# Nine norm factors spread over the partitions through DRAM instead of by TensorE, in a two-layer decoder on one core

## The chip, the core and the metric

The kernel runs on one core of a Trainium2 chip. Its metric is the device time in microseconds (us) of one execution, as a median of runs; lower is better. PE is TensorE (its matmuls; PEld its weight loads), DVE is VectorE, ACT is ScalarE, POOL is GpSimd, SP is SyncE. "Stage" below is a slab of weights of at most 1024 columns that is loaded, split and multiplied as one.

## The reference

Two layers on a sequence of 256 tokens with 2048 features, all in float32. Layer 0 mixes tokens by a state-space scan (SSD), layer 1 by attention with a forget gate (FoX). Both then have a gated feed-forward part of 5632 features and a gated extra input. Every part stands between root-mean-square norms:

```python
def rmsnorm(x, w):
    y = xf * lax.rsqrt(jnp.mean(xf * xf, axis=-1, keepdims=True) + EPS)
    return y * w
...
    y = y.reshape(b, l, SSD_D_INNER) * jax.nn.silu(z)      # SSD mixer
    yg = y.reshape(b, l, g, SSD_D_INNER // g)              # 8 groups of 512
    yg = yg * lax.rsqrt(jnp.mean(yg * yg, axis=-1, keepdims=True) + EPS)
    y = yg.reshape(b, l, SSD_D_INNER) * norm_w
    return y @ w_out
```

The change concerns nine of these norms: the eight group norms in the SSD mixer (the "gate norms", one for each group of 512 features) and the norm ahead of FoX's input product. Each has one factor per token, 256 in all.

## The kernel before, in words

Activations lie transposed, features on partitions and 256 tokens along the free dimension, as tiles of 128 x 256. All products are made to float32 precision from two float32r halves: a weight tile `raw` comes by DMA on SP's queue (L194), ACT rounds it to `wh` (L208), DVE makes the rest `wl = raw - wh` (L213), and PE makes three products for each weight block of 128 x 128 (L269 to L271, or L263 to L265 where tokens are the stationary side, as for FoX's V). Six accumulators (`acc`, in PSUM) rotate, four of them to a unit of 512 output features; two more PSUM tiles (`mi`) serve the small products.

A unit runs over its stages. After each stage one task is popped from a list `bg`, so that the small work of one unit runs beside the products of the next. In the SSD layer units alternate: `xs_unit(g+1)` makes the scan's input of group g+1 (its accumulators are read by DVE at L299 as `xr<-acc`), `z_unit(g)` makes the gate of group g (`g<-acc`, L299). `core_tasks` is the scan of a group: decays `E` on ACT (L1001, L1008) and DVE (L1009), the transposed input `xd` (DVE, L986), their products on PE (L1021). `gate_tasks` is the gate norm. The program's order on each engine is made by a scheduler from the order of the code, its own timing model and the pins `issue_after`: `after(low_a[0])` puts an instruction behind the last emitted `wh` cast, `paced` puts one behind the last emitted `wl` and ahead of the next.

A norm has three steps. `rstd_small` (L349): PE sums the squares over the partitions by using the 128 x 256 tile of squares as stationary side, 128 tokens at a time, against a column of ones (L352), which leaves the factor of token 128 j + p on partition p, column j; DVE scales it (`ms`, L355), GpSimd takes it to the power -1/2 (`rs`, L358). `rstd_wide` (L361): DVE splits the two columns into `rh` and `rl` (L363, L364), PE spreads each column over all partitions by four products of 128 columns (L368), and ACT copies the result out of PSUM (L372), for the gate norms as `grw`. Then the factors are used: for a gate norm by `gn3` (L1055), four operations of DVE that scale `y` (L1058). In `gate_tasks` the steps are `gn1`, `gn2`, `gn3`, one stage after the other; for the last two groups `gn3` is pinned and comes in the output product (`last7`, L1142). For FoX's norm the steps are made by `mk_r` (L544) and run inside V's second unit; `rwide` and `rq = rwide * FOXS` (L1266) are first used when the `q` and `k` units are read out.

Of the kernel before, what the change touches and what calls it, by code (L numbers as in the profile page):

```python
# [65 lines left out]
def tile_trunk(ctx, tc, a, out):  # L66
# [4 lines left out]
    def pool(stack, name, bufs=1, **kw):  # L71
        return stack.enter_context(tc.tile_pool(name=name, bufs=bufs, **kw))
# [10 lines left out]
    gap = pool(ctx, "gap")  # L83
    psa = pool(ctx, "psa", bufs=6, space=PSUM)
    psm = pool(ctx, "psm", bufs=2, space=PSUM)

    cnt = [0]

# [203 lines left out]
    def misc():  # L292
        return psm.tile([P, 512], F32, tag="mi", name=nm("mi"))
# [52 lines left out]
        turn.append(last_v[0])  # L346
        return r

    def rstd_small(acc, n):  # L349
        ps = misc()  # L350
        for j in range(2):
            PE.matmul(ps[:, j:j + 1], lhsT=acc[:, j * P:(j + 1) * P], rhs=ones[:, :1],  # L352
                      start=True, stop=True)
        ms = tmp("ms", (P, 2))
        dmark[0] = V.tensor_scalar(out=ms, in0=ps[:, :2], scalar1=1.0 / n, scalar2=EPS,  # L355
                                   op0=mult, op1=add)
        rs = tmp("rs", (P, 2), bufs=3)
        G.tensor_tensor(out=rs, in0=ms, in1=mhalf, op=ALU.pow)  # L358
        return rs

    def rstd_wide(rs, o):  # L361
        rr = [tmp("rh", (P, 2), F32R), tmp("rl", (P, 2), F32R)]
        V.tensor_copy(out=rr[0], in_=rs)  # L363
        dmark[0] = V.tensor_tensor(out=rr[1], in0=rs, in1=rr[0].bitcast(F32), op=sub)  # L364
        ps = misc()
        for j in range(2):
            for i in range(2):
                PE.matmul(ps[:, j * P:(j + 1) * P],  # L368
                          lhsT=rr[i][:, j:j + 1].broadcast_to((P, P)), rhs=identr,
                          start=i == 0, stop=i == 1)  # L370
        if o is not None:
            mark[0] = A.copy(out=o, in_=ps[:, :T])  # L372
        return ps[:, :T]

    def log1p_exp_neg_abs(v, new):
        ab = new()
# [164 lines left out]
                emit_stage(hi, prev[0])  # L541
        return up

    def mk_r(half=True, small=None):  # L544
        r = []

        def f1():
            r.append(rstd_small(ssb, D))
            if small is not None:
                V.tensor_copy(out=small, in_=r[0])  # L550

        def f2():
            rstd_wide(r[0], rwide)
            if half:
                V.tensor_scalar(out=rwide2, in0=rwide, scalar1=0.5, scalar2=None, op0=mult)
        return f1, f2

    def mk_r_paced():
# [266 lines left out]
    with ExitStack() as ys:  # L825
        yp = pool(ys, "yp", side="right")
        y = [yp.tile([P, T], F32, name=f"y{c}") for c in range(32)]
        with ExitStack() as st:
# [136 lines left out]
            def core_tasks(g, xg):  # L965
# [26 lines left out]
                def decay(q, half):  # L992
                    h0 = 8 * g + 4 * q
                    ab = S[f"a{q}"]
                    if half == 0:
                        S[f"E{q}"] = s3[0].tile([P, 4, 384], F32, tag="E", name=nm("E"), bufs=2)
                    E = S[f"E{q}"]
                    with after(low_a[0]):
                        for i in range(2 * half, 2 * half + 2):
                            for b, lo in ((0, 0), (1, P), (2, P)):  # L1000
                                A.activation(E[:, i, b * P:(b + 1) * P], ab[:, i, lo:lo + P],  # L1001
                                             AF.Relu, scale=-1.0,
                                             bias=bias3[:, b, h0 + i:h0 + i + 1])
# [35 lines left out]
                def ymm_y():  # L1039
                    ymm()  # L1040
                    y_of(1)

                return [lambda: decay(0, 0), lambda: decay(0, 1), xpose, lambda: decay2(0),
                        lambda: decay(1, 0), lambda: decay(1, 1), lambda: decay2(1), noop, ymm_y,
                        lambda: y_of(0), noop]

            def gate_tasks(g, S):
                def gn1():
                    S["rs"] = rstd_small(S["ss"], 512)

                def gn2():
                    S["rw"] = yp.tile([P, T], F32, tag="grw", name=nm("grw"), bufs=1)
                    rstd_wide(S["rs"], S["rw"])

                def gn3():  # L1055
                    for c in range(4):
                        yc = y[4 * g + c]
                        last_v[0] = V.scalar_tensor_tensor(out=yc, in0=yc, scalar=col("ssd_norm", 4 * g + c),  # L1058
                                               in1=S["rw"], op0=mult, op1=mult)
                if g < NG - 2:  # L1060
                    return [noop, gn1, gn2, gn3]
                late.append(lambda: paced(gn3))
                return [noop, gn1, gn2] if g < NG - 1 else [gn1, noop, gn2, noop]

            xgs, late, later, last7 = {}, [], [], []
            zt = {}

            def z_a(t):
# [41 lines left out]
            def z_unit(g, pops):  # L1110
                S = {}

                def ev_z(t, acc):
                    if t == 0:
                        while len(bg) > left[0]:
                            bg.popleft()()
                    if t == 0:
                        S["ss"] = ssp
                        if g == 0:
                            gated(0, z00, z00)  # L1120
                    if g == 0:
                        t += 1
                    yc = y[4 * g + t]
                    if g == NG - 1:
                        later.append((acc, yc, S["ss"]))
                        return
                    z = tmp("g0")
                    gated(t, acc, z)

                def gated(t, src, z):  # L1130
                    yc = y[4 * g + t]
                    gather_with(src, z, rwide2)
                    th = tmp("th")
                    A.activation(th, z, AF.Tanh)
                    V.scalar_tensor_tensor(out=z, in0=th, scalar=1.0, in1=z, op0=add, op1=mult)
                    V.tensor_tensor(out=yc, in0=yc, in1=z, op=mult)
                    sumsq(S["ss"], yc, t == 0)
                unit(lambda k: xs0[k], ev_z, pops=pops)
                if g < NG - 1:
                    bg.extend(gate_tasks(g, S))  # L1140
                else:
                    last7.extend([late[0]] + gate_tasks(g, S) + [late[1]])  # L1142

            xs_unit(0)
            for g in range(NG - 1):
# [10 lines left out]
                bg.append(lambda c=c: ysplit(c))  # L1156
            left[0] = 0
            z_unit(NG - 1, 2)
        xq_s = ExitStack()
        xq = pool(xq_s, "xq", bufs=16)  # L1160
        zp = pool(xq_s, "zp")
# [4 lines left out]
            later[t] = (z, yc, ss)  # L1166
        turn.append(took[0][1])
        low[0] = took[0][1]
        bg.extend([lambda j=j: z_step(j) for j in range(6)] + last7)
        st0 = {}  # L1170

        def m0():
# [79 lines left out]
                            in1=bigm.unsqueeze(1).broadcast_to((P, 4, P)), op=add)  # L1252
        return ck

    v1, v2 = mk_r(False, rsm)

    def both(t, acc):
        if t == 0:
# [3 lines left out]
    for u in range(1, 5):  # L1262
        unit(lambda k: nxt[k], both if u == 1 else ev_v(u), tok=True,
             late=(lambda: (drain(), v1()), v2) if u == 1 else ())
        if u == 1:
            V.tensor_scalar(out=rq, in0=rwide, scalar1=float(FOXS), scalar2=None, op0=mult)  # L1266
    bg.extend((f1, noop, f2, noop, f3))
    ots = {}

# [177 lines left out]
```

## Time and profile before

| what | before |
|---|---|
| median of 3 runs | 2702.18 us (2701.43 to 2702.31) |
| the profiled execution | 2703.08 us, its span 2701.3 us |
| PE busy | 2695.0 us, 23302 matmuls |
| DVE, ACT, POOL busy | 1782.0, 1395.5, 46.7 us |
| granted TensorE clock | full (1.000) |
| DMA queues: SP's; GpSimd's; ACT's | 504.54 MB; 12.15 MB; 0.14 MB |

The span runs from the first instruction to the last; the execution has some 2 us around it. A float32 product that is not float32r (L352, L1021) leaves two records for each matmul. Matmuls overlap in the trace, so that their cost is read from start to start, and not from their durations.

### The profile page before, as it was taken

What the parts mean: (1) busy time and instruction counts of PE and PEld (TensorE: products, weight loads), DVE (VectorE), ACT (ScalarE), POOL (GpSimd) and SP (SyncE); (2) the same over time, 40 slices, a digit from 0 to 9 for tenths busy, and PEclk for the clock granted to TensorE, in tenths of its full rate; (3) what the DMA queues carried; (4) which work ended last, traced back from release to release, by engine and by line L of the source; (5) the groups of instructions that cost most, each with busy time, mean ns of one, the idle gap of its engine ahead of it and who ended that gap; (6) DMA issues with size and microseconds to landing.
All of it is one profiled execution on the core that took longest, in us unless ns stands there. A gap on an engine that the chain in (4) does not pass through costs nothing. (4 is left out here: it accounts for less than half of the span.)

```text
span 2701.3 us, 56196 instructions
## 1 busy us (share of the span) xinstructions
PE 2695.0 (100%) x23302; PEld 2679.6 (99%) x23302; DVE 1782.0 (66%) x2747; ACT 1395.5 (52%) x2156; POOL 46.7 (2%) x108
## 2 busy tenths in 40 slices
PE   9999999999999999999999999999999999999999
PEld 9999999999999999999999999999999999999999
DVE  8788888754966545666568656656865545656577
ACT  6577666554644444444446544455644444444455
POOL 0000000000000000000000000000000000000000
PEclk9999999999999999999999999999999999999999
DMA  7666666565666666666656676655766666666655
GB/s 267 188 205 200 191 195 190 161 216 172 193 205 195 193 193 193 195 178 203 200 164 209 183 224 185 179 159 173 204 203 194 195 195 193 193 179 210 195 166 171
DMA packets 262736, 520.42 MB, mean 193 GB/s; under 512 B 17440, under 2 KB 44224, under 8 KB 262480
## 3 DMA queue, kind: packets, MB, share of 16 engines
q1 hardware_dynamic: 258784, 504.54, 62.3%
q0 software_dynamic: 3552, 12.15, 1.5%
q8 instruction: 182, 2.98, 0.4%
q14 instruction: 74, 0.61, 0.1%
q10 hardware_dynamic: 144, 0.14, 0.0%
HBM read 514.58 MB, written 2.18 MB: 191 GB/s over the span
## 5 line engine op out<-in xcount | busy, mean ns | idle before, releaser
L213 DVE TENSOR_TENSOR wl<-raw,wh 128x1024 fp32r<-128x1024 f32 (+4 forms) x1020 | 1173.2, 1152 | 751.1 <-ACT wh L208 749.8
L208 ACT CAST wh<-raw 128x1024 fp32r<-128x1024 f32 (+4 forms) x1020 | 1011.3, 994 | 1116.8 <-PE acc L270 991.4
L270 PE MATMUL acc<-x,wh 128*128 128x256 f32 x5120 | 1392.0, 277 | 0.0
L271 PE MATMUL acc<-x,wl 128*128 128x256 f32 x5120 | 1365.3, 276 | 0.0
L269 PE MATMUL acc<-x,wh 128*128 128x256 f32 x5120 | 1356.9, 277 | 0.0
L270 PEld LDWEIGHTS acc<-x,wh 128*128 128x128 f32 x5120 | 960.9, 188 | 2.1 <-issue 1.9
L271 PEld LDWEIGHTS acc<-x,wl 128*128 128x128 f32 x5120 | 948.3, 188 | 0.8 <-issue 0.7
L269 PEld LDWEIGHTS acc<-x,wh 128*128 128x128 f32 x5120 | 936.7, 188 | 1.1 <-issue 0.9
L270 PE MATMUL acc<-a,wh 128*128 128x256 f32 x1408 | 388.2, 276 | 0.0
L269 PE MATMUL acc<-a,wh 128*128 128x256 f32 x1408 | 388.0, 276 | 0.0
L271 PE MATMUL acc<-a,wl 128*128 128x256 f32 x1408 | 385.4, 275 | 0.0
L270 PEld LDWEIGHTS acc<-a,wh 128*128 128x128 f32 x1408 | 264.4, 188 | 0.0
L269 PEld LDWEIGHTS acc<-a,wh 128*128 128x128 f32 x1408 | 264.2, 188 | 0.0
L271 PEld LDWEIGHTS acc<-a,wl 128*128 128x128 f32 x1408 | 263.5, 188 | 0.0
L269 PE MATMUL acc<-xb,wh 128*128 128x256 f32 x512 | 143.8, 281 | 0.5 <-DVE qk L299 0.5
L270 PE MATMUL acc<-xb,wh 128*128 128x256 f32 x512 | 141.4, 276 | 0.0
L271 PE MATMUL acc<-xb,wl 128*128 128x256 f32 x512 | 140.6, 276 | 0.0
L269 PEld LDWEIGHTS acc<-xb,wh 128*128 128x128 f32 x512 | 96.1, 188 | 1.2 <-DVE qk L299 0.9
L270 PEld LDWEIGHTS acc<-xb,wh 128*128 128x128 f32 x512 | 96.2, 188 | 0.2
L271 PEld LDWEIGHTS acc<-xb,wl 128*128 128x128 f32 x512 | 95.8, 188 | 0.2 <-issue 0.2
L917 DVE SCALAR_TENSOR_TENSOR g<-xr,vec,g 128x256 f32<-128x256 f32 x144 | 66.3, 478 | 8.5 <-ACT g L914 7.9
L269 PE MATMUL acc<-xq,wh 128*128 128x256 f32 x256 | 70.7, 276 | 0.0
(217 smaller groups left out, 1979.4 us busy)
## 6 DMA issues: line engine op xcount, KB each, us to landing
raw<-down SPq DMA_DIRECT2D x176, 512.0 KB, 3.7
raw<-ssd_in SPq DMA_DIRECT2D x144, 512.0 KB, 4.2
raw<-gate SPq DMA_DIRECT2D x128, 512.0 KB, 3.7
raw<-up SPq DMA_DIRECT2D x128, 512.0 KB, 3.7
raw<-fox_in SPq DMA_DIRECT2D x64, 512.0 KB, 4.2
raw<-gate SPq DMA_DIRECT2D x64, 384.0 KB, 3.3
raw<-up SPq DMA_DIRECT2D x64, 384.0 KB, 3.6
raw<-ssd_out SPq DMA_DIRECT2D x40, 512.0 KB, 3.7
```

The lines of the kernel that those rows point to most:

```text
L208: low_a[0] = A.copy(out=wh, in_=raw)
L213: low[0] = V.tensor_tensor(out=wl, in0=raw, in1=wh.bitcast(F32), op=sub)
L269: PE.matmul(o, lhsT=w, rhs=x[:, 0, :], start=st, stop=False)
L270: PE.matmul(o, lhsT=w, rhs=x[:, 1, :], start=False, stop=False)
L271: last = PE.matmul(o, lhsT=wl[:, c, t * P:(t + 1) * P], rhs=x[:, 0, :], start=False, stop=sp)
L917: V.scalar_tensor_tensor(out=c, in0=xr[:, k:k + T], scalar=col(f"conv_w{k}", cc), in1=c, op0=mult, op1=add)
```

## The change

The factors of the nine norms no longer go through PE, DVE's split and ACT's copy. GpSimd writes the two columns of `rs` to a scratch tile in DRAM behind the power (`sent`), and ACT's DMA queue fetches them from there to all 128 partitions (`fetched`), pinned behind a `wh` cast. The scalings `gn3` are pinned as well. `gn2` and `gn3` of a group are put on a second list `scale`, from which `core_tasks` of a later group takes one entry at its fourth and one at its eighth step.

```diff
-    def rstd_small(acc, n):
+    def rstd_small(acc, n, woven=False):
         ps = misc()
+        if woven:
+            halves_ = acc.rearrange("p (q j) -> p j q", j=2)
+        else:
+            halves_ = acc.rearrange("p (j q) -> p j q", j=2)
         for j in range(2):
-            PE.matmul(ps[:, j:j + 1], lhsT=acc[:, j * P:(j + 1) * P], rhs=ones[:, :1],
+            PE.matmul(ps[:, j:j + 1], lhsT=halves_[:, j, :], rhs=ones[:, :1],
                       start=True, stop=True)
...
+    def sent(rs, woven):
+        d = rp.tile([2 * P], F32, tag="rsd", name=nm("rsd"), bufs=2)
+        G.dma_start(out=d.rearrange("(p j) -> p j" if woven else "(j p) -> p j", j=2), in_=rs)
+        return d
+
+    def fetched(d, o):
+        with after(low_a[0]):
+            A.dma_start(out=o, in_=d.partition_broadcast(P))
...
-                return [lambda: decay(0, 0), lambda: decay(0, 1), xpose, lambda: decay2(0),
-                        lambda: decay(1, 0), lambda: decay(1, 1), lambda: decay2(1), noop, ymm_y,
+                return [lambda: decay(0, 0), lambda: decay(0, 1), xpose,
+                        lambda: (next_scale(), decay2(0)),
+                        lambda: decay(1, 0), lambda: decay(1, 1), lambda: decay2(1), next_scale, ymm_y,
                         lambda: y_of(0), noop]
...
                 def gn1():
-                    S["rs"] = rstd_small(S["ss"], 512)
+                    S["rs"] = sent(rstd_small(S["ss"], 512, True), True)
...
-                    rstd_wide(S["rs"], S["rw"])
+                    fetched(S["rs"], S["rw"])
...
                 if g < NG - 2:
-                    return [noop, gn1, gn2, gn3]
-                late.append(lambda: paced(gn3))
-                return [noop, gn1, gn2] if g < NG - 1 else [gn1, noop, gn2, noop]
+                    return [noop, gn1, lambda: scale.extend((gn2, lambda: paced(gn3))), noop]
+                late.append((gn2, lambda: paced(gn3)))
+                return [noop, gn1, noop] if g < NG - 1 else [gn1]
...
-                    last7.extend([late[0]] + gate_tasks(g, S) + [late[1]])
+                    last7.extend([late[0][1]] + gate_tasks(g, S) + [noop] * 4
+                                 + [late[1][0]] + [noop] * 3 + [late[1][1]])
...
-        bg.extend([lambda j=j: z_step(j) for j in range(6)] + last7)
+        bg.extend([lambda j=j: (z_step(j), late[0][0]() if j == 1 else None)
+                   for j in range(6)] + last7)
...
-    v1, v2 = mk_r(False, rsm)
+    def v2():
+        rs_v.append(sent(rs_v[0], False))
+
+    def scale_q():
+        last_v[0] = V.tensor_scalar(out=rq, in0=rwide, scalar1=float(FOXS), scalar2=None, op0=mult)
...
         if u == 1:
-            V.tensor_scalar(out=rq, in0=rwide, scalar1=float(FOXS), scalar2=None, op0=mult)
+            bg.extend([noop] * 5 + [lambda: fetched(rs_v[1], rwide)] + [noop] * 4
+                      + [lambda: paced(scale_q)])
```

With `woven` the stationary side of L352 takes every second token, so that the factor of token 2 p + j stands on partition p, column j, and a partition's two factors lie side by side in DRAM.

The scheduler orders the SSD layer's instructions anew. PE's queue has 36 matmuls fewer (the nine calls of L368), and its other rows keep their number. The products with `E` and `xd` of the fifth group stand behind 2921 plain products in the changed order, and behind 2911 before. Lines of the changed kernel are numbered up to 30 higher.

ACT's queue, fifth gate norm. `wh` is a stage's cast, `E` the decays, `th` and `g` belong to the convolution of the next group. Before, the copy of the factors stands among the casts:

```order
L208 CAST wh_5505<-raw_5503 128x1024
L208 CAST wh_5539<-raw_5537 128x1024
L372 COPY grw_5492<-mi_5497 128x256
L208 CAST wh_5621<-raw_5619 128x1024
L1001 ACTIVATE E_5649<-ab_5611,bias_219 128x128 x6
L914 ACTIVATE g_423_5570<-xr_5567,vec 128x256
```

In the changed order the fetch stands later in the same unit, ahead of the exponential:

```order
L209 CAST wh_5655<-raw_5653 128x1024
L931 ACTIVATE th_5536<-g_412_5531 128x256
L931 ACTIVATE th_5547<-g_415_5542 128x256
L209 CAST wh_5698<-raw_5696 128x1024
L387 DMA grw_5726<-rsd_5436 128x256
L1019 ACTIVATE E_5610<-E_5610 128x1536
L925 ACTIVATE g_418_5553<-xr_5550,vec 128x256
```

An issue on ACT's queue has taken the place of the copy, and it moved from the head of the unit to its middle, between a cast and the exponential.

DVE's queue at the end of that unit, where the `z` accumulators are read (`g<-acc`) and `xd` is made. Before:

```order
L921 SCALAR_TENSOR_TENSOR xg_5278<-th_5608,g_432_5603 128x256
L213 TENSOR_TENSOR wl_5875<-raw_5872,wh_5874 128x1024
L299 TENSOR_TENSOR g_445_5902<-acc_5615,rwide_159 128x256
L213 TENSOR_TENSOR wl_5947<-raw_5944,wh_5946 128x1024
L299 TENSOR_TENSOR g_447_5909<-acc_5616,rwide_159 128x256
L1135 SCALAR_TENSOR_TENSOR g_445_5902<-th_5904,g_445_5902 128x256
L986 TENSOR_TENSOR xd_5722<-mi_5723,rpe 128x512
L213 TENSOR_TENSOR wl_5997<-raw_5994,wh_5996 128x1024
L986 TENSOR_TENSOR xd_5722<-mi_5724,rpe 128x512
```

In the changed order:

```order
L214 TENSOR_TENSOR wl_5838<-raw_5835,wh_5837 128x1024
L1070 SCALAR_TENSOR_TENSOR y_199<-y_199,vec,grw_5726 128x256
L1070 SCALAR_TENSOR_TENSOR y_200<-y_200,vec,grw_5726 128x256
L1070 SCALAR_TENSOR_TENSOR y_201<-y_201,vec,grw_5726 128x256
L1070 SCALAR_TENSOR_TENSOR y_202<-y_202,vec,grw_5726 128x256
L300 TENSOR_TENSOR g_435_5869<-acc_5576,rwide_161 128x256
L214 TENSOR_TENSOR wl_5914<-raw_5911,wh_5913 128x1024
L300 TENSOR_TENSOR g_437_5876<-acc_5577,rwide_161 128x256
L997 TENSOR_TENSOR xd_5683<-mi_5684,rpe 128x512
L214 TENSOR_TENSOR wl_5964<-raw_5961,wh_5963 128x1024
L997 TENSOR_TENSOR xd_5683<-mi_5685,rpe 128x512
```

The four scalings `gn3`, which stood ahead of the reads `xr<-acc` at the head of the unit before, now stand ahead of the reads `g<-acc`, and one operation on `g` (L1135) went behind `xd`.

ACT's queue at the start of the output product, seventh gate norm, where the fetch stands closest behind its norm's sums (there `ms` stands in DVE's queue behind the second `wl` of 768 columns). Before:

```order
L208 CAST wh_6829<-raw_6827 128x768
L208 CAST wh_6859<-raw_6857 128x768
L372 COPY grw_6690<-mi_6695 128x256
L208 CAST wh_6912<-raw_6910 128x768
L312 CAST x_6916<-y_183 128x256
L1070 ACTIVATE th_6937<-z_0_6896 128x256
```

In the changed order:

```order
L209 CAST wh_6863<-raw_6861 128x768
L313 CAST x_6867<-y_185 128x256
L1086 ACTIVATE th_6888<-z_0_6847 128x256
L1086 ACTIVATE th_6920<-z_1_6849 128x256
L209 CAST wh_6892<-raw_6890 128x768
L313 CAST x_6896<-y_186 128x256
L387 DMA grw_6922<-rsd_6620 128x256
L209 CAST wh_6926<-raw_6924 128x768
```

Here the fetch stands behind the fourth cast of 768 columns, two behind the one whose rest `wl` the sums follow.

More of the change, by code (lines that the diff above doesn't have):

```diff
@@ L85, in tile_trunk @@
     psm = pool(ctx, "psm", bufs=2, space=PSUM)
+    rp = pool(ctx, "rp", space=bass.MemoryType.DRAM)
     cnt = [0]
@@ L542, in mk_update, with mk_r @@
         return up
-    def mk_r(half=True, small=None):
+    def mk_r():
         r = []
@@ L548, in f1 @@
             r.append(rstd_small(ssb, D))
-            if small is not None:
-                V.tensor_copy(out=small, in_=r[0])
         def f2():
             rstd_wide(r[0], rwide)
-            if half:
-                V.tensor_scalar(out=rwide2, in0=rwide, scalar1=0.5, scalar2=None, op0=mult)
+            V.tensor_scalar(out=rwide2, in0=rwide, scalar1=0.5, scalar2=None, op0=mult)
         return f1, f2
@@ L1060, in gate_tasks, with next_scale @@
                 if g < NG - 2:
-                    return [noop, gn1, gn2, gn3]
-                late.append(lambda: paced(gn3))
-                return [noop, gn1, gn2] if g < NG - 1 else [gn1, noop, gn2, noop]
-            xgs, late, later, last7 = {}, [], [], []
+                    return [noop, gn1, lambda: scale.extend((gn2, lambda: paced(gn3))), noop]
+                late.append((gn2, lambda: paced(gn3)))
+                return [noop, gn1, noop] if g < NG - 1 else [gn1]
+            def next_scale():
+                if scale:
+                    scale.popleft()()
+            xgs, late, later, last7, scale = {}, [], [], [], deque()
             zt = {}
@@ L1158, in tile_trunk @@
             z_unit(NG - 1, 2)
+            assert not scale
         xq_s = ExitStack()
@@ L1253, in load_ck, with v1 @@
         return ck
-    v1, v2 = mk_r(False, rsm)
+    rs_v = []
+    def v1():
+        rs_v.append(rstd_small(ssb, D))
+        V.tensor_copy(out=rsm, in_=rs_v[0])
+    def v2():
+        rs_v.append(sent(rs_v[0], False))
+    def scale_q():
+        last_v[0] = V.tensor_scalar(out=rq, in0=rwide, scalar1=float(FOXS), scalar2=None, op0=mult)
     def both(t, acc):
```

## The prediction

> **What bounds the kernel now.** I read the page's shares first, then the waits of PE, then busy time by stretch, then single rows of the timeline.
>
> ```profile
> span 2701.3 us, 56196 instructions
> PE 2695.0 (100%) x23302; PEld 2679.6 (99%) x23302; DVE 1782.0 (66%) x2747; ACT 1395.5 (52%) x2156; POOL 46.7 (2%) x108
> ```
>
> PE is busy for all but 6.3 us of the span. Its waits, over the whole run (what waited, for whom, us in total, times, longest):
>
> ```profile
> PE mi L419 <- DVE mhalf L401: 1.1, 1, 1.1
> PE acc L269 <- DVE qk L299: 0.5, 2, 0.3
> PE mi L352 <- DVE ssb L322: 0.3, 2, 0.2
> ```
>
> That is 1.9 us in all, the first of it ahead of the first product. The busy time by stretch (us, PE, PEld, DVE, ACT, POOL, then the clock, the DMA share, GB/s), once for the stretch that the change works in and once for a stretch of plain weight products behind it:
>
> ```profile
> 180.00:520.00 340.00, 340.00 (x3017) 332.22 (x3017) 278.36 (x474) 221.69 (x403) 14.31 (x40) 1.00 0.63 189
> 560.00:660.00 100.00, 100.00 (x885) 100.00 (x884) 50.93 (x52) 47.28 (x64) 0.00 (x0) 1.00 0.65 196
> ```
>
> PE never stops in either, at full clock. So the time is the sum of what stands in PE's queue. DVE is busy 82% of the first stretch (278.36 of 340) and ACT 65%: idle time there is worth nothing as long as PE is fed. A plain product costs 100 us / 885 = 0.113 us from start to start; its "duration" of 0.28 us below is pipelined and is not its cost.
>
> **The change, part by part.** *What leaves PE.* Each of the nine removed calls of `rstd_wide` issues four products at L368. One call for a gate norm, with its neighbours:
>
> ```profile
> 392.67 0.28 PE L270 MATMUL acc<-x,wh 128*128 128x256 f32 x1
> 392.79 0.22 PE L368 MATMUL mi<-identr,rh 128*128 128x128 f32 x1
> 392.85 0.33 PE L271 MATMUL acc<-x,wl 128*128 128x256 f32 x1
> 393.02 0.22 PE L368 MATMUL mi<-identr,rl 128*128 128x128 f32 x1
> 393.08 0.27 PE L368 MATMUL mi<-identr,rh 128*128 128x128 f32 x1
> 393.19 0.28 PE L368 MATMUL mi<-identr,rl 128*128 128x128 f32 x1
> 393.30 0.33 PE L269 MATMUL acc<-x,wh 128*128 128x256 f32 x1
> 393.47 0.28 PE L270 MATMUL acc<-x,wh 128*128 128x256 f32 x1
> 393.59 0.28 PE L271 MATMUL acc<-x,wl 128*128 128x256 f32 x1
> ```
>
> From 392.67 to 393.59 are 0.92 us with eight spacings, four of them those of plain products. Without the four of L368, 4 x 0.113 = 0.45 would be left, so one call costs PE 0.47 us. All eight gate norms have this form, so they give 8 x 0.47 = 3.7 us. The ninth call stands among the wider products of V:
>
> ```profile
> 1532.95 0.35 PE L264 MATMUL acc<-wl,xb 128*128 128x412 f32 x1
> ...
> 1533.77 0.35 PE L263 MATMUL acc<-wh,xb 128*128 128x412 f32 x1
> ...
> 1534.89 0.35 PE L263 MATMUL acc<-wh,xb 128*128 128x412 f32 x1
> ```
>
> The last six spacings (1533.77 to 1534.89) take 1.12 us, 0.187 each. From 1532.95 to 1533.77 two such spacings and the four of L368 take 0.82, so the call costs 0.82 - 0.37 = 0.45 us. Sum: 3.7 + 0.45 = 4.2 us, all on the path, because PE is the path. The 36 products come to 4.2 / 36 = 0.116 us each, as much as a plain product of twice the columns. The Trainium skill, page "TensorE: Matmul & The Clock Gate", section "Back-to-back issue gap", gives about 81 ns per matmul of 128 columns in a stream with weight loads; by that the 36 would be worth 2.9 us and the time 2699.3. The rows above differ from it, and the sum goes by the rows.
>
> *What PE keeps, in another form.* `rstd_small` still makes its two products for each norm, but for the eight gate norms it now reads its stationary operand with a step of two elements.
>
> ```profile
> 387.91 0.28 PE L271 MATMUL acc<-x,wl 128*128 128x256 f32 x1
> 388.02 0.50 PE L352 MATMUL mi<-ones,ssp 128*128 128x1 f32 x4
> 388.38 0.36 PE L269 MATMUL acc<-x,wh 128*128 128x256 f32 x1
> 388.58 0.28 PE L270 MATMUL acc<-x,wh 128*128 128x256 f32 x1
> L352 PEld LDWEIGHTS mi<-ones,ssp 128*128 128x128 f32 x40 | 5.3, 190 | 0.0
> L368 PEld LDWEIGHTS mi<-identr,rh 128*128 128x128 f32 x36 | 6.8, 188 | 0.4 <-PE mi L861 0.4
> ```
>
> Today one call (four records) takes 0.67 - 2 x 0.113 = 0.44 us. No load of before has a step of two, so bounds: nothing more, or all of it doubles, 8 x 0.44 = 3.5 us. The nearest row is the L368 load: it reads one column 128 times, a step of zero, and takes 188 ns against 190 for the step of one. The step made no difference there, so I take zero; the 3.5 us are a rival. A gain from the step is excluded, since the same four loads remain.
>
> *What moves on ACT.* Nine copies go, nine DMA issues come:
>
> ```profile
> L372 ACT COPY grw<-mi x8: 348/374/374, 211.0 to 517.0; 128x256 f32<-128x256 f32 x8
> 0.74 0.41 ACTq L408 DMA_DIRECT2D h<-x  x1
> ```
>
> 0.37 against 0.41 us: 0.04 more for each, but the copy stood in a gap of ACT's, and the issue stands ahead of the big exponential (L1008). Behind each issue are queued the casts `wh` of the next stages, and PE waits for those. The fetch itself waits for the write of `rsd`, below.
>
> *What moves on DVE.* Eighteen operations of two columns go. The four scalings of `gn3` move from the head of an `xs` unit to just ahead of the accumulator reads of a `z` unit. Who waits behind them: PE, for the accumulators and then for `xd`, whose products (L1021) are next. The tightest case of before (DVE rows, then PE):
>
> ```profile
> 393.91 1.67 DVE L1058 SCALAR_TENSOR_TENSOR y<-y,vec,grw 128x256 f32<-128x256 f32 x4 [0.31 <-ACT grw L372]
> 419.50 0.41 DVE L1135 SCALAR_TENSOR_TENSOR g<-th,g 128x256 f32<-128x256 f32 x1
> 421.63 0.68 DVE L986 TENSOR_TENSOR xd<-mi,rpe 128x512 f32<-128x512 f32 x1
> 423.44 0.65 PE L1021 MATMUL mi<-E,xd 128*64 128x256 f32 x4
> ```
>
> `xd` is done at 422.31, 1.13 us before PE takes it. The change puts 1.67 us of `gn3` ahead of it and moves L1135 (0.41) behind; with ACT's 0.41 in the chain that feeds DVE, it is at worst 1.67 us later. In the changed order PE has 10 more plain products ahead of these (2921 against 2911 for this group), 10 x 0.113 = 1.1 us. Left: 1.13 + 1.1 - 1.67 = 0.6 us. So PE does not wait, and the move costs nothing; without this cover it costs up to 1.67 us in each of seven groups. That it may cost less than nothing is excluded, because PE does not wait there now.
>
> *What is new: write and fetch.* GpSimd takes the power, then issues the write; behind it stand the `xr` fills and the `ab` loads. ACT's fetch waits for the landing.
>
> ```profile
> L358 POOL TENSOR_TENSOR rs<-ms,mhalf x18: 692/1276/1602, 33.6 to 2652.1; 128x2 f32<-128x2 f32 x18
> L970 POOL DMA_DIRECT2D ab<-acd x16 | 8.8, 548 | 44.3 <-ACT E L1001 37.3 <-PE mi L943 5.7 <-ACT g L914 0.8
> acd<-acT POOLq DMA_DIRECT2D x1, 64.0 KB, 3.3
> h<-x ACTq DMA_DIRECT2D x1, 136.0 KB, 3.7
> 490.02 0.96 DVE L213 TENSOR_TENSOR wl<-raw,wh 128x768 fp32r<-128x768 f32 x1 [1.91 <-ACT wh L208]
> 495.86 0.40 ACT L312 CAST x<-y 128x256 fp32r<-128x256 f32 x1
> 498.17 0.84 ACT L208 CAST wh<-raw 128x768 fp32r<-128x768 f32 x1 [1.92 <-issue]
> ```
>
> On POOL, 0.55 us of issue nine times, on an engine that is busy 2%: nothing. The write's landing is bounded by the one store to DRAM shown here, 3.3 us from issue (for 64 times its bytes, though not in pieces of 8 bytes). A stage of weights is 18 to 24 plain products, 2.0 to 2.7 us at 0.113. In eight of the nine cases the fetch stands four to six stages behind the norm's sums, 8 us or more. The closest is the seventh gate norm, at the start of the output product: `ms` there stands behind the DVE row at 490.02, so it is done near 491.2, the power near 492.5, the landing near 495.8; the fetch stands behind ACT's row that ends at 496.26. ACT's next cast began only at 498.17, so even a landing 2.4 us late hides. Nothing again. The fetch moves as much as ACT's one load of before, which landed 3.7 us after its issue; its readers stand two stages of 2.7 us behind it or more. The ninth result is read only by the first `q` unit, three units on.
>
> *The sum* against the profiled execution (2703.1 us, of it 2701.3 span): 2703.1 - 4.2 = 2698.9. The median of the runs is 2702.2, 0.9 below; the same 4.2 off it gives **2698.0 us**, 0.16% less. A measurement of this kernel can tell about 0.2% (5.4 us) from no change, so this counts as no change.
>
> **The rivals.** *Strided weights cost double.* Against it stand the two load rows; for it, only that no row has this step. It takes 3.5 of the 4.2 us back: 2701.5.
>
> *PE waits for `xd` (the other side).* Place: L1021 behind L986 behind `gn3`, in seven groups. Price: 7 x (lateness beyond 0.6 us). For it: DVE is 82% busy in that stretch, and one product with `cbm` more in front would do it. If DVE comes 1.7 us late beyond my worst case, PE loses 7 x 1.1 = 7.7 us: 2698.0 + 7.7 = 2705.7, slower than before; it passes before's time from 1.2 us late, and 0.2% over it from 2.0. Against it: DVE gets the 1.67 us back earlier in the same unit, where `gn3` stood.
>
> *The fetch stands on ACT.* Place: the seventh gate norm. The landing must be more than 2.4 us late before ACT's casts slip at all, and PE has the casts already made to live on; a landing 10 us after issue would shift them by 10 - 3.3 - 2.4 = 4.3 us and cost PE 0 to 4 us, once: 2698 to 2702. For it: no row of before shows a store in pieces of 8 bytes, nor one beside a DVE that is 82% busy. The Trainium skill, page "SBUF — State Buffer", section "SBUF: two separate sides", speaks against the change here: in some of its operations DVE holds the port pair that it shares with GpSimd, GpSimd then can't write the descriptors of its DMA, and the DMA starts late. No run shows that so far; by this rule the landing is late by the rest of one DVE operation, which the 2.4 us would mostly take up.
>
> *More is gained*: the 0.5 us wait at L269 for `qk` closes too: 2697.5.
>
> **How the numbers follow.** The forecast and small errors of it, 0.76; strided weights 0.10; `xd` 0.09; the fetch 0.05. Faster by over 0.2% would need 5.4 us, more than all that leaves PE: 0.08, out of the forecast's share, for a size misread. Slower by over 0.2%: half of `xd` and a part of the fetch, 0.08. Within 0.2%: 0.84. The range goes from 2696.8 (2697.5 with the wait closed, less the 0.7 us by which the lowest of the three runs lies under their median) to 2702.1 (strided weights 2701.5, the fetch at its worst 2702, and the 0.1 us by which the highest run lies over the median); it leaves out most of `xd` and what is beyond.
>
> **What would show it.** Right: 36 matmuls fewer, PE's waits as above, PE's busy time near 2690.8. The strided rival: the call of `rstd_small` takes 0.88 us instead of 0.44. The `xd` rival: waits of PE's products with `E` and `xd` for DVE. The fetch rival: ACT idle ahead of the fetch, released by the DMA of `rsd`, and PE waiting for `wh` near 500 us. Wrong altogether: a new wait of PE of over a microsecond that none of these names.

## The result, and the profile after

The changed kernel takes 2698.27 us in the median of 22 runs, the kernel before 2702.97 in 22 runs beside it: the ratio is 0.9983 with a 95% interval of 0.9977 to 0.9989, or 4.7 us less (3.0 to 6.2). The forecast was 2698.0 and 4.2 us less. The 0.17% lies within the 0.2% that the prediction took for no change, but these runs do tell it from none: the interval ends 3.0 us short of it. One of the 22 runs, the one profiled first, was disturbed (14217.5 us), so the profile shown here is that of the first experiment, the same kernel again at 2697.82 us against 2703.08 before.

The page of the changed kernel, span and PE:

```profile
span 2696.0 us, 56125 instructions
PE 2689.8 (100%) x23266; PEld 2674.2 (99%) x23266; DVE 1779.5 (66%) x2729; ACT 1395.4 (52%) x2147; POOL 52.5 (2%) x117
```

There are 36 matmuls fewer. PE's busy time is 5.2 us less (the prediction had 4.2), and PE stands for 6.2 us of the span, where it was 6.3. PE's waits over the whole run (who, for whom, us in total, times, longest):

```profile
PE mi L433 <- DVE mhalf L415: 1.1, 1, 1.1
PE acc L270 <- ACT wh L209: 0.8, 1, 0.8
PE mi L357 <- DVE ssb L323: 0.3, 2, 0.2
```

The middle one is new in this run and lies at 9.6 us, long ahead of the change's first place. The 0.5 us for `qk` is gone. No wait names `xd`, `grw` or `rsd`.

To see where the 5.3 us of the span came from, take the same piece of work in both traces. PE's sum of squares (`rstd_small`) of the first gate norm, of the norm behind the SSD layer, of FoX's norm and of the one behind FoX, first before (start, duration), then after:

```profile
201.49 0.28 PE L352 MATMUL mi<-ones,ssp 128*128 128x1 f32 x2
671.42 0.28 PE L352 MATMUL mi<-ones,ssb 128*128 128x1 f32 x2
1527.88 0.39 PE L352 MATMUL mi<-ones,ssb 128*128 128x1 f32 x3
1875.09 0.28 PE L352 MATMUL mi<-ones,ssb 128*128 128x1 f32 x2
```

```profile
201.88 0.29 PE L357 MATMUL mi<-ones,ssp 128*128 128x1 f32 x2
668.20 0.28 PE L357 MATMUL mi<-ones,ssb 128*128 128x1 f32 x2
1524.70 0.39 PE L357 MATMUL mi<-ones,ssb 128*128 128x1 f32 x3
1870.23 0.39 PE L357 MATMUL mi<-ones,ssb 128*128 128x1 f32 x3
```

The stretch with the eight gate norms took 469.93 us and takes 466.32: 3.61 less. The stretch behind it, 671.42 to 1527.88 before, has none of the nine and takes 856.46 and 856.50. FoX's stretch went from 347.21 to 345.53, 1.68 less. By the prediction's price the ninth call is 0.45 of it, and the closed wait for `qk` is 0.5; these rows do not explain the other 0.7.

The call of `rstd_small` with weights read in steps of two, with its neighbours (as quoted in the prediction for before):

```profile
386.34 0.28 PE L272 MATMUL acc<-x,wl 128*128 128x256 f32 x1
386.46 0.52 PE L357 MATMUL mi<-ones,ssp 128*128 128x1 f32 x4
386.84 0.36 PE L270 MATMUL acc<-x,wh 128*128 128x256 f32 x1
387.04 0.28 PE L271 MATMUL acc<-x,wh 128*128 128x256 f32 x1
```

386.34 to 387.04 are 0.70 us, less two plain spacings 0.47, where it was 0.44. The eight calls thus give back 0.2 us of the 3.7, which leaves 3.5 to set against the measured 3.61. The median weight load of this kind takes 196 ns, where it was 191.

In the same group `gn3` runs ahead of `xd` (two rows of DVE, then PE's product that needs it; only three of the four scalings are in the first row):

```profile
415.79 1.27 DVE L1070 SCALAR_TENSOR_TENSOR y<-y,vec,grw 128x256 f32<-128x256 f32 x3
420.51 0.69 DVE L997 TENSOR_TENSOR xd<-mi,rpe 128x512 f32<-128x512 f32 x1
422.55 0.65 PE L1032 MATMUL mi<-E,xd 128*64 128x256 f32 x4
```

`xd` is done at 421.20, 1.35 us before PE takes it; before the change these were 1.13. In the trace `gn3` stands right ahead of `xd` or inside it in four groups, and `xd` has 1.3 to 1.9 us to spare there.

And the tightest fetch, at the seventh gate norm (GpSimd's write, ACT with the fetch on its queue), with the landing times of all nine writes:

```profile
489.40 0.59 POOL L382 DMA_DIRECT2D rsd<-rs  x1 [0.30 <-POOL rs L363]
```

```profile
493.12 0.40 ACT L313 CAST x<-y 128x256 fp32r<-128x256 f32 x1
493.45 0.33 ACTq L387 DMA_DIRECT2D grw<-rsd  x1
495.43 0.84 ACT L209 CAST wh<-raw 128x768 fp32r<-128x768 f32 x1 [1.92 <-PE acc L271]
```

```profile
L382 POOL DMA_DIRECT2D rsd<-rs x9: 582/592/758, 203.9 to 1526.6; - x9
DMA to landing us min/median/max: 4.0/4.5/8.4
```

The write landed 4.0 us after 489.40, just as ACT came to the fetch, and ACT's next cast waited for PE until 495.43 anyhow. At the eighth norm and at FoX's the landing came last too: their fetches were issued 0.03 and 0.02 us after it (517.33 and 1534.96), and no wait of PE followed. The 8.4 us are the landing of FoX's write, the one that still goes out in pieces of 4 bytes.

### The profile page after: what moved, and what is told of

It is laid out like the page before. It is cut to its first block, busy times and chain, and to the rows that moved or that the text cites. A ratio compares the mean times of both kernels' runs of the same rounds, so it can differ in the third digit from the quotient of the medians.

```text
span 14215.8 us, 56125 instructions
## 1 busy us (share of the span) xinstructions
PE 14210.8 (100%) x23266; PEld 13989.9 (98%) x23266; DVE 1815.1 (13%) x2729; ACT 1406.6 (10%) x2147; POOL 56.9 (0%) x117
## 4 chain that ended last, share of the span: by engine, by line
PE 100%; DVE 0%; ACT 0%; issue 0%
PE acc L272 31%; PE acc L270 31%; PE acc L271 31%; PE acc L264 1%; PE acc L266 1%; PE acc L265 1%; PE mi L1032 1%; PE mi L1359 0%; PE mi L1311 0%; PE mi L991 0%; PE acc L469 0%; PE acc L472 0%; PE acc L473 0%; PE mi L357 0%; PE mi L1343 0%; PE mi L954 0%
## 5 line engine op out<-in xcount | busy, mean ns | idle before, releaser
L271 PE MATMUL acc<-x,wh 128*128 128x256 f32 x5120 | 4896.3, 957 | 0.0
L272 PE MATMUL acc<-x,wl 128*128 128x256 f32 x5120 | 4839.1, 959 | 0.0
L270 PE MATMUL acc<-x,wh 128*128 128x256 f32 x5120 | 4797.2, 960 | 0.0
L271 PEld LDWEIGHTS acc<-x,wh 128*128 128x128 f32 x5120 | 4478.4, 876 | 4.8 <-issue 4.8
L272 PEld LDWEIGHTS acc<-x,wl 128*128 128x128 f32 x5120 | 4418.3, 874 | 10.1 <-issue 10.1
L270 PEld LDWEIGHTS acc<-x,wh 128*128 128x128 f32 x5120 | 4390.3, 875 | 11.6 <-issue 9.5
L270 PE MATMUL acc<-a,wh 128*128 128x256 f32 x1408 | 1214.2, 863 | 0.0
L272 PE MATMUL acc<-a,wl 128*128 128x256 f32 x1408 | 1211.3, 863 | 0.0
L271 PE MATMUL acc<-a,wh 128*128 128x256 f32 x1408 | 1206.1, 857 | 0.0
L270 PEld LDWEIGHTS acc<-a,wh 128*128 128x128 f32 x1408 | 1097.3, 780 | 0.0
L271 PEld LDWEIGHTS acc<-a,wh 128*128 128x128 f32 x1408 | 1097.2, 779 | 0.0
L272 PEld LDWEIGHTS acc<-a,wl 128*128 128x128 f32 x1408 | 1085.3, 773 | 0.0
L270 PE MATMUL acc<-xb,wh 128*128 128x256 f32 x512 | 540.5, 1056 | 0.0
L271 PE MATMUL acc<-xb,wh 128*128 128x256 f32 x512 | 528.9, 1033 | 0.0
L270 PEld LDWEIGHTS acc<-xb,wh 128*128 128x128 f32 x512 | 483.1, 944 | 3.9 <-issue 3.9
L271 PEld LDWEIGHTS acc<-xb,wh 128*128 128x128 f32 x512 | 483.5, 944 | 2.6 <-issue 2.6
```

The costliest lines, as they stand in the source:

```text
L270: PE.matmul(o, lhsT=w, rhs=x[:, 0, :], start=st, stop=False)
L271: PE.matmul(o, lhsT=w, rhs=x[:, 1, :], start=False, stop=False)
L272: last = PE.matmul(o, lhsT=wl[:, c, t * P:(t + 1) * P], rhs=x[:, 0, :], start=False, stop=sp)
```

## The experiments

Each time is a median of runs on one chip beside runs of the kernel before (2702.7 to 2703.3 us); "the changed kernel" stands at 2698.56. The name in brackets is the one that the expectations use.

### The changed kernel again (again)

> The changed kernel itself, for a profile of an undisturbed run and a second set of times. My theory (36 products off PE's path at 0.116 us each, all else covered): 4.2 us under before, PE busy 4.2 us less than 2695.0, PE's waits as before, no wait of PE for xd; the call of rstd_small with the step of two costs 0.44 us of PE as before. The strided-weights theory: that call costs 0.88 us. The xd theory: waits of PE's products with E and xd for DVE. The fetch theory: ACT idle ahead of the fetch near 500 us and PE waiting for wh there.

Measured: 2698.56 us, ratio 0.9983 (0.9974 to 0.9992). It is the profile above: no wait for `xd`, no fetch for which PE waits, a strided call at 0.47 and not 0.88 us.

### The same nine factors by PE, at the new places (late_products)

```diff
-                    S["rs"] = sent(rstd_small(S["ss"], 512, True), True)
+                    S["rs"] = rstd_small(S["ss"], 512)
...
-                    fetched(S["rs"], S["rw"])
+                    rstd_wide(S["rs"], S["rw"])
```

and likewise for FoX's norm.

> The changed kernel with the nine factors spread by TensorE again, at the places where the changed kernel fetches them (the later scalings stay where the change put them; nothing goes through DRAM). My theory, that only the 36 products count and the moves are free: the time of before, 2703 us, 4.2 above the changed kernel, and 0.46 us of PE a call. A theory that the moved scalings are worth something by themselves: the time lies off that of before by that much; if the gain came from the moves alone, it stays at the changed kernel's time.

Measured: 2703.64 us, ratio to before 1.0002 (0.9993 to 1.0011), 5.1 above the changed kernel. So the moves alone gain nothing, and the gain hangs on taking the products off PE. But the comparison is not clean. PE's waits between 200 and 560 us, where the changed kernel has none:

```profile
PE mi L991 <- DVE xg L932: 0.8, 1, 0.8
PE acc L272 <- DVE wl L214: 0.6, 1, 0.6
PE mi L373 <- DVE xd L997: 0.3, 1, 0.3
```

The gate norms' stretch takes 471.21 us here, 4.9 more than in the changed kernel, and 1.7 of them are these waits. The other 3.2 go to the products (3.5 by their price). Less the waits the stretch is 0.4 us shorter than before the change, so the moves by themselves gain no more than that.

### Sixteen products for each norm (sixteen)

```diff
     def fetched(d, o):
+        ps = misc()
+        for k in range(16):
+            PE.matmul(ps[:, k % 2 * P:(k % 2 + 1) * P], lhsT=identr, rhs=identr,
+                      start=True, stop=True)
         with after(low_a[0]):
```

> The changed kernel with 16 products of 128 columns (identity by identity, result unread) put on PE at each of the nine fetches, 144 in all, to price such a product in PE's stream. My theory, 0.116 us each: 16.7 us above the changed kernel. By the skill's 81 ns each (Trainium skill, TensorE: Matmul & The Clock Gate, Back-to-back issue gap): 11.7 us above. A theory that PE has slack somewhere in the stretch: less than either.

Measured: 2714.17 us, ratio 1.004 (1.0028 to 1.0053), 15.6 us above the changed kernel. PE at the first of the nine:

```profile
225.74 0.28 PE L272 MATMUL acc<-x,wl 128*128 128x256 f32 x1
225.85 1.90 PE L388 MATMUL mi<-identr 128*128 128x128 f32 x16
227.59 0.34 PE L270 MATMUL acc<-x,wh 128*128 128x256 f32 x1
227.76 0.28 PE L271 MATMUL acc<-x,wh 128*128 128x256 f32 x1
```

225.74 to 227.76 are 2.02 us; less two plain spacings 1.79, or 0.112 each. 144 of them make 16.1 us; the two medians differ by 15.6 (0.108 each) and the two profiled spans by 16.6, a wait of 0.5 us for `qk` among them. So a product of 128 columns costs PE nearly as much as one of 256 (0.113) in this stream, not the 81 ns of the expectation's other theory, and PE has no slack in which it could hide.

### Weights in steps of one, and 4-byte pieces (straight)

```diff
-                    S["rs"] = sent(rstd_small(S["ss"], 512, True), True)
+                    S["rs"] = sent(rstd_small(S["ss"], 512), False)
```

With steps of one the two factors on a partition belong to tokens that lie 128 apart, so the write to DRAM goes out in 256 pieces of 4 bytes instead of 128 of 8.

> The changed kernel with the gate norms' stationary operand read in steps of one again; the write to DRAM then goes out in pieces of 4 bytes instead of 8. My theory: the step of two costs nothing and a longer landing is covered, so the time of the changed kernel within 0.1%, and the call of rstd_small takes 0.44 us in both. The strided-weights theory: 3.5 us (0.13%) faster than the changed kernel, with 0.44 against 0.88 us a call. A theory that the landing is near its limit: slower, with ACT idle ahead of some fetch.

Measured: 2707.38 us, ratio to before 1.0013 (1.0005 to 1.0022): slower than before, and 8.8 us slower than the changed kernel. Neither the first nor the second theory holds; the third does. The landings of the writes (the trace holds four of the nine), PE's waits for ACT and DVE, and ACT at the seventh gate norm:

```profile
DMA to landing us min/median/max: 8.6/9.7/11.1
```

```profile
PE acc L270 <- ACT x L313: 5.2, 2, 3.8
PE acc L270 <- DVE qk L300: 2.0, 2, 1.5
PE acc L271 <- DVE x L315: 1.4, 2, 1.0
```

```profile
492.30 0.40 ACT L313 CAST x<-y 128x256 fp32r<-128x256 f32 x1
499.55 0.33 ACTq L387 DMA_DIRECT2D grw<-rsd  x1
499.99 0.83 ACT L209 CAST wh<-raw 128x768 fp32r<-128x768 f32 x1 [7.29 <-PE acc L272]
```

ACT stands 7.29 us at the fetch. The releaser printed is PE, which had long been done; what came last is the landing of `rsd`, which let the fetch go at 499.55. At the eighth it stands 9.71 us. Behind the fetches are queued the casts `x` of the output product's operands, and PE waits for those:

```profile
501.18 0.38 PE L270 MATMUL acc<-x,wh 128*128 128x256 f32 x1 [1.43 <-ACT x L313]
529.45 0.58 PE L270 MATMUL acc<-x,wh 128*128 128x256 f32 x1 [3.81 <-ACT x L313]
```

From start to start PE loses 3.0 us at the seventh norm (499.47 to 502.76 for three spacings) and 7.0 at the eighth (525.36 to 534.87 for 22). At the seventh that is two waits, 2.4 us in all, and 0.6 around them. At the eighth the waits are 4.25 us, and most of the rest is the clock (the row has the form of the busy times by stretch in the prediction; the clock is the figure 0.50):

```profile
528.00:534.80 6.80, 4.92 (x21) 4.62 (x22) 5.68 (x11) 4.79 (x9) 0.00 (x0) 0.50 0.78 172
```

The granted clock stands at half for these 6.8 us, which begin 1.4 us before the wait ends, and plain products come every 0.213 us in them instead of every 0.113.

This is the prediction's rival of the fetch, at the place that it named and at the eighth norm too. What keeps the changed kernel out of it is the step of two, which I had taken for something with only a cost. The profile also has 2.7 us more in FoX's stretch, 2.0 of it the wait for `qk`.

### 4-byte pieces for the first six only (six_straight)

```diff
-                    S["rs"] = sent(rstd_small(S["ss"], 512, True), True)
+                    S["rs"] = sent(rstd_small(S["ss"], 512, g >= NG - 2), g >= NG - 2)
```

> The changed kernel with steps of one and 4-byte pieces for the first six gate norms only; the last two keep their steps of two and 8-byte pieces. My theory, that 4-byte pieces only cost where the fetch stands close behind the write (the last two): landing 9 to 11 us six times, no wait of PE from it, the changed kernel's time within 1.5 us. A theory that the 4-byte pieces as such load the DMA engines or GpSimd and so slow the rest: six eighths of the 9 us, 2705. A theory that the first six pay alone: near 2707.

Measured: 2697.41 us, ratio 0.998 (0.9971 to 0.9989), no different from the changed kernel. The trace holds the landings of two of the six writes in 4-byte pieces, 8.7 and 9.1 us. The slow writes cost nothing where the fetch stands further behind, and PE does not wait between 200 and 560 us. So what `straight` lost there belongs to the last two norms.

### The fetch right behind the write (fetch_now)

```diff
                     S["rs"] = sent(rstd_small(S["ss"], 512, True), True)
+                    S["rw"] = yp.tile([P, T], F32, tag="grw", name=nm("grw"), bufs=1)
+                    fetched(S["rs"], S["rw"])
```

and `gn2` is left empty.

> The changed kernel with the eight gate norms' fetches issued right behind their writes instead of two to five stages later. My theory, that the distance between write and fetch is what keeps ACT free: ACT stands at each of the eight fetches until the write has landed, some 5 to 7 us (0.72 us power, 0.30 gap, 4.0 to 6.9 landing), and by what a stand of 6.9 us cost PE with steps of one and 4-byte pieces (2.8 us at one place, 5.1 at another), eight of them cost 16 to 40 us: 2714 to 2738. A theory that PE lives on the casts already made, so that the place of the fetch does not matter: the changed kernel's time within 3 us.

Measured: 2698.23 us, ratio 0.9984 (0.9975 to 0.9993): my theory missed by some 16 us, and the place of the fetch does not matter with 8-byte pieces. ACT at the seventh norm:

```profile
492.47 0.33 ACTq L387 DMA_DIRECT2D grw<-rsd  x1
492.85 0.42 ACT L1087 ACTIVATE th<-z 128x256 f32<-128x256 f32 x1 [2.44 <-DMA rsd<-rs]
```

ACT stands 2.44 us here and 2.3 or less at the others, since it gets to the fetch late and the gate norms' writes land 3.7 to 4.3 us after issue. PE does not wait between 200 and 560 us: it lives through that on the casts already made.

### The fetch right behind the write, with 4-byte pieces (now_straight)

The edits of `straight` and `fetch_now` together: `sent(rstd_small(S["ss"], 512), False)` with the fetch behind it.

> Fetches right behind their writes, as in fetch_now, but with 4-byte pieces, which landed 8.3 to 11.1 us after issue. My theory, that ACT may stand 2.4 us at a fetch without loss and pays beyond 2.7 to 4.1 us: stands of 5.4 to 7.3 us (the 0.9 to 2.4 of fetch_now and 4.5 to 4.9 us of later landing) at eight places, 1.3 to 4.6 us of PE each, so 10 to 37 us over the changed kernel, 2708 to 2735, with PE waiting for wh or for tiles that ACT makes. A theory that only the two places at the output product are touchy: some 9 us over it, 2707.

Measured: 2742.56 us, ratio 1.0147 (1.0133 to 1.0161), 44 us over the changed kernel, a little beyond the first theory's range and far from the second's. ACT's waits for the write (in the eighth place the 7.3 us are put down to PE again), and the landings (six of the nine):

```profile
ACT wh L209 <- DMA rsd<-rs: 27.0, 3, 9.8
ACT E L1012 <- DMA rsd<-rs: 24.2, 3, 9.0
ACT th L1087 <- DMA rsd<-rs: 7.6, 1, 7.6
ACT wh L209 <- PE acc L272: 7.3, 1, 7.3
```

```profile
DMA to landing us min/median/max: 8.8/10.5/11.9
```

The stands sum to 66.1 us in eight places, 8.3 each, longer than I had worked out because the writes landed later. In the profile, which is 48.3 us longer than the changed kernel's, PE waits 30.4 us between 200 and 570 us, where the changed kernel has no wait. Half of it (15.0 us) is for accumulators that DVE reads late (`xr<-acc`), which the expectation did not name, and 5.0 are for `wh`. The granted clock is 0.96 on average there:

```profile
200.00:570.00 370.00, 339.55 (x2852) 329.16 (x2852) 262.58 (x437) 210.47 (x389) 20.60 (x48) 0.96 0.66 166
```

The clock stands at half in eight stretches of 3.4 or 6.8 us, 34.0 us in all, which is up to 17 us of work. So a stand cost 3.8 us of waiting and up to 2.1 by the clock. By the waits alone 4.5 us of each stand were covered by casts already made; in the run with 4-byte pieces it was 4.9 of 7.29 us and 5.5 of 9.71. A stand of ACT of 2.4 us cost nothing. Where in between PE begins to wait, these runs do not show, and once PE waits for long the clock adds to the price.

### Twice as many pieces of 8 bytes (twice)

```diff
-        d = rp.tile([2 * P], F32, tag="rsd", name=nm("rsd"), bufs=2)
-        G.dma_start(out=d.rearrange("(p j) -> p j" if woven else "(j p) -> p j", j=2), in_=rs)
-        return d
+        d = rp.tile([2, 2 * P], F32, tag="rsd", name=nm("rsd"), bufs=2)
+        if woven:
+            G.dma_start(out=d.rearrange("k (p j) -> p k j", j=2),
+                        in_=rs.unsqueeze(1).broadcast_to((P, 2, 2)))
...
+        return d[0]
```

> The changed kernel with each gate norm's factor written twice, 256 pieces of 8 bytes instead of 128; the second copy is read by nobody. If the landing goes by the number of pieces: 8 to 11 us as with 256 pieces of 4 bytes, ACT stands 5 to 9 us at the last two fetches, and the time is near 2707. If it goes by the size of a piece (4 bytes slow, 8 bytes quick): 4 to 5 us, and the changed kernel's time, 2698.

Measured: 2697.76 us, ratio 0.9981 (0.9972 to 0.999), the changed kernel's time. The eight doubled writes:

```profile
L383 POOL DMA_DIRECT2D rsd<-rs x8: 739/758/763, 203.5 to 510.9; - x8
DMA to landing us min/median/max: 4.3/4.6/4.8
```

The number of pieces sets GpSimd's issue (758 ns for 256, 592 for 128), but not the landing: 256 pieces of 8 bytes land in 4.6 us, 256 of 4 bytes in 8.6 us or more. Of the two it is the size of the piece that counts, or the layout in DRAM that goes with it: no run has the one without the other.

### More work on DVE ahead of `xd` (xd_eight, xd_four)

```diff
+                    for c in range(8 if g < NG - 2 else 0):
+                        last_v[0] = V.scalar_tensor_tensor(out=spare, in0=y[4 * g + c % 4],
+                                               scalar=col("ssd_norm", 4 * g),
+                                               in1=S["rw"], op0=mult, op1=mult)
```

> The changed kernel with eight more scalings of 128x256 on DVE behind each of the first six moved ones, into a tile that nothing reads, 8 x 0.42 = 3.3 us of DVE ahead of xd. By the slack that the profile of the changed kernel shows (1.34 to 1.35 us in three groups, 1.93 in one, 8 or more in the others): 3 x 2.0 + 1.4 = 7.4 us slower, with PE waiting for xd there. By the 0.6 us of the prediction in seven groups: 7 x 2.7 = 19 us slower. By a theory that DVE has the room to spare at 82%: no change.

Measured: 2710.97 us, ratio 1.0032 (1.002 to 1.0043), 12.4 us over the changed kernel. PE's waits in it:

```profile
PE acc L272 <- DVE wl L214: 6.4, 5, 1.7
PE mi L992 <- DVE xg L933: 3.3, 1, 3.3
```

PE waits for DVE, but not for `xd`, and the run does not put the rival to the test as meant: in three groups the scheduler put `xd` ahead of all but one of the added scalings. What came late is the next `wl`, and once `xg` (whose transposes PE makes). In the last of the six groups all eight stand ahead of `xd`, and there it was ready only 0.2 us before PE took it. The wait of 3.3 us was followed by 3.4 us at half clock, as in the run with 4-byte pieces.

With `range(4 ...)` in the same place:

> The changed kernel with four more scalings of 128x256 on DVE behind each of the first six moved ones, 4 x 0.42 = 1.7 us each. With eight of them PE waited for wl, not for xd: 1.86 us three times and 1.0 once, so DVE had 3.3 - 1.86 = 1.5 us to spare in three groups and 2.3 in one. By that: 3 x 0.2 us, and less than 1.5 us over the changed kernel. By the 0.6 us to xd of the prediction: 7 x 1.1 = 7.7 us over it. By a loss in proportion (half of the 12.7 us that eight cost): 6.4 us.

Measured: 2701.33 us, ratio 0.9997 (0.9988 to 1.0006), 2.8 us over the changed kernel: more than the first theory gives, less than the others.

```profile
PE acc L272 <- DVE wl L214: 2.5, 1, 2.5
```

One wait, for `wl` in the last of the six groups, makes up that difference in the SSD layer; in the other groups PE does not wait, as the first theory has it. (The profile also has 1.3 us of waits for `qk`.) The single wait was not foreseen. In the changed kernel a `wl` stands right behind `gn3` there (457.18); with the added work the next one comes 7 us behind it (461.41 against 454.25), an order that the added work itself changed.

### Four more norms (more)

```diff
-                r.append(rstd_small(ssb, D))
+                r.append(sent(rstd_small(ssb, D, True), True))
...
-                r.append(rstd_wide(r[0], None))
+            fetched(r[0], rwide)
...
-        return f1, f2, noop, f3
+        return f1, noop, noop, f2, noop, noop, f3
```

and the same for the gated extra input (`pe_small`, `pe_wide`), whose sums move ahead by two stages.

> The changed kernel with four more norms' factors through DRAM in the same way: the two of the per-layer gate (their sums moved two stages ahead to make room) and the two late ones of the feed-forward (three stages more between sums and use, the tanh steps in pairs). 16 more products leave PE, 0.46 us a call. My theory, all else covered: 1.8 us under the changed kernel, 2696.5, PE busy 1.8 us less. A theory that the stages behind it have no room left for the landing (4 to 5 us for the write and as much for the fetch): equal or slower, with PE waiting for operands that come from the scaled tiles.

Measured: 2711.46 us, ratio 1.0031 (1.0019 to 1.0043), 13 us over the changed kernel: the second theory. ACT at the first of the two late norms, and PE behind it:

```profile
729.22 2.31 ACT L209 CAST wh<-raw 128x768 fp32r<-128x768 f32 x3 [5.16 <-DMA rsd<-rs]
```

```profile
740.08 0.45 PE L272 MATMUL acc<-x,wl 128*128 128x256 f32 x1 [2.38 <-DVE wl L214]
```

ACT stands 5.16 us at the fetch, then makes three `wh` in a row; DVE in turn stands 2.24 us until the fetch itself has landed (733.29), and PE (second row) waits 2.38 us for a `wl` behind that. At the four fetches ACT stands 5.2, 3.3, 4.7 and 4.1 us. PE waits 11.9 us in the whole profile, where the changed kernel has 2.2: 2.6 behind the first fetch and 4.1 behind the third, each with 3.4 us at half clock, 1.2 behind the second, and nothing behind the fourth. So what a stand costs depends on the place and not on its length alone. This version does not beat the changed kernel, and neither does any other run by more than its interval.

## Why the prediction was right, step by step

**The products.** Right. The gate norms' stretch gives 3.61 us where 3.7 stood (3.5 with the step of two), FoX's stretch has room for the 0.45, and the kernel with the products put back stands at the time of before, with 1.7 us of new waits in it. The price that decided was that of the rows: the 144 products of `sixteen` cost 0.108 to 0.112 us each, where the Trainium skill, page "TensorE: Matmul & The Clock Gate", section "Back-to-back issue gap", has about 81 ns; by that the eight norms would have given 2.6. That the median came within 0.3 us of the forecast is in part luck: before took 0.8 us more in the 22 runs than in the three that the forecast started from, and the gain was 0.5 us larger than forecast.

**The step of two** was taken at nothing and costs 0.03 us a call, 0.2 in all. The rival that doubled the call is out. But the step was costed on PE alone: its other end is the write, where it makes 8-byte pieces of 4-byte ones, and without it the change is slower than before. That term was missing from the sum; the forecast came out because the change happened to have it, and not because the prediction had reckoned with it.

**The write and the fetch.** The landing at the seventh norm was put at 3.3 us after issue, by a store of 64 KB, and measured 4.0; the eight gate norms' writes took 4.0 to 6.9. The landing was thought to have 2.4 us to spare ahead of ACT's next cast, and had 2.0 (493.4 to 495.43). The fetches of the eight took 4.3 to 6.5 us to land, where 3.7 stood. "Nothing" was right. But at the eighth and ninth norms, which the prediction had put among the safe ones, the fetch too was issued only as its write landed. The rival that ACT stands at the fetch was right in its mechanism and its place, and its condition was not met. Its price was too small: with the landing near 10 us, 0 to 4 us "once" became 3.0 and 7.0 us in the profile (8.8 in all by the medians), because the eighth norm's fetch stands close behind its write too, and I had counted only one; and because a wait of PE costs more than its length, by the half clock that came with it.

The Trainium skill's rule on the port that DVE shares with GpSimd (page "SBUF — State Buffer", section "SBUF: two separate sides") would show as writes that start late beside a busy DVE. GpSimd's issue took 582 to 595 ns for the eight gate norms, but a landing varied from 4.0 to 6.9 us with no cause that I could read; no run here parts the port from the DMA behind it, so the rule is neither shown nor refuted.

**`xd`.** Right that PE does not wait; the 0.6 us to spare were 1.35, and four groups have `gn3` at this place, not seven. The bound charged all 1.67 us of the moved scalings to `xd`, although DVE had time ahead of them to take them up: in the changed kernel it idles 1.8 us between 394.5 and 415.4 us. Where DVE was made late, PE waited for `wl` or `xg` first; once, in `late_products`, it waited 0.3 us for `xd` as well. In no run was `xd` itself much later than this, so the rival's price stays untested.

**The `qk` wait.** Its 0.5 us are gone in the profile, as the last rival had it, and it was worth more than 0.5. In the five runs without this wait (the changed kernel, `fetch_now`, `six_straight`, `twice`, `xd_eight`) FoX's stretch takes 345.5 to 345.9 us; before takes 347.21, or 346.76 without the ninth call. So some 1.2 us of the profile's 5.3 go with the wait, and the products account for the rest. But the kernel with the products put back shows the same wait at 0.8 us and the one with 4-byte pieces at 2.0, so it moves with everything that shifts FoX's stages. Whether the change closes it as a rule stays open; by the runs, the gain is 4.7 us against the 4.2 forecast, and its interval (3.0 to 6.2) holds the sum with the closed wait and without.

## What to carry to other kernels

When an engine is busy for the whole span, take small products off it by their spacing from start to start, not by their size, and pay for it with latency elsewhere only where the queue that carries the wait has slack: here ACT could stand 2.4 us for nothing, and at stands of 7 to 10 us PE waited for what was beyond 4.5 to 5.5. Read the clock along with the waits: a long wait of the busy engine also cost a stretch at half clock. An access pattern has two ends: a step that looks like a cost on the reading side may be what makes the pieces of a DMA twice as large. Before extending a change that works, look at the distance between write and fetch at each new place, since the same edit gained where ACT came to the fetch as the write landed, and lost where it came 5 us earlier.

## What the runs showed of the hardware

- GpSimd's write to DRAM in 256 pieces of 4 bytes landed 7.5 to 11.9 us after issue over all runs (where a trace holds the landing), in 128 pieces of 8 bytes 3.1 to 7.7 us, and 256 pieces of 8 bytes landed as fast (4.3 to 4.8) as 128.
- GpSimd's issue of such a DMA took 0.59 us for 128 pieces and 0.76 for 256, whichever their size.
- A weight load that reads float32 in steps of two costs 5 to 7 ns more than one in steps of one (median load 196 against 191 ns; 0.47 against 0.44 us for a call of four).
- All five waits of PE of 3.3 us or more (3.3 to 5.8, in `straight`, `now_straight` and `xd_eight`) came with a stretch of 3.4 or 6.8 us at half clock, in which plain products came every 0.213 us instead of 0.113. Of shorter waits some did (2.4 us in `more`) and some did not (2.5 us in `xd_four`).
